# Query projection in 512 columns, and the last two groups' heads taken by token tile

## The chip, the core and the metric

The kernel runs on one core of a Trainium2 chip. The metric is the device time of one execution in microseconds. Before the change it was run three times: 1211.14, 1211.49 and 1213.31, median 1211.49. The engines are called as in the profile: PE is TensorE (matmuls; PEld its weight loads), DVE is VectorE, ACT is ScalarE, POOL is GpSimd, SP is SyncE, which issues the loads from memory.

## The reference

A two-layer decoder trunk on 512 tokens of width 1024: one mLSTM layer, then one layer of sliding-window attention with 16 query heads in 4 key-value groups, each followed by a squared-ReLU MLP and a gated embedding. The change touches the attention layer alone:

```python
def swa_sink_attention(x, pos, k_sh, v_sh, w_q, b_q, sinks, w_o, b_o):
    B, S, _ = x.shape
    nb = S // WINDOW                                    # WINDOW = 128, nb = 4
    q = partial_rope((x @ w_q + b_q).reshape(B, S, A_Q_HEADS, A_HEAD_DIM), pos)
    q = q.reshape(B, nb, WINDOW, A_KV_HEADS, A_GROUP, A_HEAD_DIM)
    kb, vb = banded(k_sh, nb), banded(v_sh, nb)
    scores = jnp.einsum('bnqkgd,bnskd->bnkgqs', q, kb).astype(jnp.float32) * (A_HEAD_DIM ** -0.5)
    ...
    m = jnp.maximum(jnp.max(scores, axis=-1), sink)
    e = jnp.exp(scores - m[..., None])
    probs = e / (jnp.sum(e, axis=-1) + jnp.exp(sink - m))[..., None]
    out = jnp.einsum('bnkgqs,bnskd->bnqkgd', probs.astype(x.dtype), vb).reshape(B, S, D_MODEL)
    return out @ w_o + b_o
```

A group has 4 query heads of 64 channels, so the queries of one group are 256 columns of x @ w_q. A token sees the 128 tokens up to itself, hence the key-value blocks of its own tile of 128 tokens and of the one before.

## The kernel before, in words

Every matrix is kept as two parts: a high part, rounded to a format that TensorE reads in one pass (`hi`), and the residue (`lo`). A product of two such matrices is three matmuls, high by high, high by low and low by high; `mm3` issues them from lines 88, 89 and 90, so that nearly all matmuls of the kernel carry those lines. A weight block of 128 x 1024 numbers (512 KB) is loaded by SyncE into one of three buffers `wraw`; ScalarE casts it to the high part (line 76) and VectorE subtracts to get the low part (line 77). Such a "split" goes into one of six buffer pairs `whi`/`wlo`.

The 512 tokens are four token tiles t = 0 to 3. The layer's input lies transposed in `XH` and `XL` (high and low), 8 blocks k of 128 channels. The attention stage runs as follows.

- Keys and values: `proj512(t, w)` takes 8 blocks x 3 matmuls of 512 columns per tile. VectorE adds the bias, rotates the keys, and four transposes through the only `tp` bank bring the keys to `KH`/`KL`.
- Queries: `q_group(gi, t, w)` does the same for one group with 256 columns. VectorE adds the bias (line 844), GpSimd rotates (lines 791 to 794), two transposes (line 848) follow, and the result goes to `QS`, which holds each head's queries as high and low part, by ScalarE copies (line 853) and VectorE subtractions (line 854).
- `attend(gi, t)`, called an attend below: 8 score matmuls into two of three `sc` banks (lines 865, 866), mask (DVE, 870), maximum (871), exponentials (ACT, 884), normalization (DVE, 888), four transposes (PE, 892), cast and residue of the probabilities `ah`, `al` (ACT 896, DVE 897), for t > 0 a triangular cut of both on GpSimd (904), then 6 (t = 0) or 12 value matmuls into a `pt` bank, and the result written over the group's queries in `QS` (ACT 915, DVE 916).
- The output projection `w_o(t, half, w)`: 24 matmuls of 512 columns per tile and half, then the residual addition (line 153) and statistics (943). The weights of the first half go into `XH` and `XL`, which can be overwritten only when the last query projection has read them; those of the second half into `whi`/`wlo`.

In the code, the four query tiles of group gi + 1 stand behind the four attends of group gi; the first half of `w_o` stands with the attends of the last group, the second half behind all attends. The emitted order is not that of the code: the framework's scheduler reorders the instructions of each engine, within what data and buffers allow, and each engine then works through its own list strictly in order. Lines 117 to 133, 141 and 145 belong to the layer norm and transposes that follow.

Of the kernel before, what the change touches and what calls it, by code (L numbers as in the profile page):

```python
# [10 lines left out]
F32 = mybir.dt.float32  # L11
# [34 lines left out]
def yoco_kernel(ctx: ExitStack, tc: tile.TileContext, A: dict, out: bass.AP):  # L46
    nc = tc.nc
    V, ACT, PE, GP = nc.vector, nc.scalar, nc.tensor, nc.gpsimd
# [30 lines left out]
    def load_w(src, n, room=None):  # L79
        raw = wpool.tile([P, 1024], F32, tag="raw", name="wraw", bufs=3)  # L80
        hi, lo = (room.tile([P, 1024], F32R, tag=f"x{x}", name=f"x{x}", bufs=4) if room else
                  wpool.tile([P, 1024], F32R, tag=f"w{x}", name=f"w{x}", bufs=6) for x in ("hi", "lo"))
        nc.sync.dma_start(raw[:, :n], src)
        split(raw[:, :n], n, hi[:, :n], lo[:, :n])
        return hi, lo

    def mm3(o, lh, ll, rh, rl, start, stop):
        PE.matmul(o, lh, rh, start=start, stop=False)  # L88
        PE.matmul(o, lh, rl, start=False, stop=False)  # L89
        PE.matmul(o, ll, rh, start=False, stop=stop)  # L90
# [18 lines left out]
    def tsl(t):  # L109
        return slice(t * P, (t + 1) * P)  # L110
# [647 lines left out]
    bq = pk.tile([P, D], F32, name="bq")  # L758
# [25 lines left out]
    pb = pool("pb", stack=bctx, side="right", reuse_waits="tile")  # L784
    def rope(x, t, nh, eng):
        tr = x[:, :, 0:ROPE].rearrange("p h (a j) -> p h a j", a=2)
        ca = cos[:, t, :].unsqueeze(1).unsqueeze(1).broadcast_to([P, nh, 2, HALF])
        sa = sin[:, t, :].unsqueeze(1).unsqueeze(1).broadcast_to([P, nh, 2, HALF])
        ta = pb.tile([P, KVH, 2, HALF], F32, tag="ta", name="ta", bufs=2)[:, :nh]
        tb = pb.tile([P, KVH, 2, HALF], F32, tag="tb", name="tb", bufs=2)[:, :nh]  # L790
        eng.tensor_mul(ta, tr, ca)
        eng.tensor_mul(tb, tr, sa)
        eng.tensor_sub(tr[:, :, 0, :], ta[:, :, 0, :], tb[:, :, 1, :])
        eng.tensor_add(tr[:, :, 1, :], ta[:, :, 1, :], tb[:, :, 0, :])
# [9 lines left out]
    w = [load_w(A["w_kv"][0, c], 1024) for c in range(4)]  # L804
# [5 lines left out]
    for t in range(NT):  # L810
        ps = proj512(t, w)
# [6 lines left out]
        pt = tp_bank()  # L818
        for h in range(KVH):
            PE.transpose(pt[:, tsl(h)], kd[:, h].rearrange("p a d -> p (a d)"), ident)  # L820
        pv = pt.rearrange("p (h s) -> p h s", s=P)
# [8 lines left out]
            put_v(vstep[t], dv)  # L830
        vlast = v

    qbank = [None]

    def q_group(gi, t, w):
        if t % 2 == 0:
            qbank[0] = mm_bank()
        ps = qbank[0][:, (t % 2) * 256:(t % 2 + 1) * 256]
        for k in range(KD):
            wh, wl = w[k // 4]  # L840
            sl = slice((k % 4) * 256, (k % 4 + 1) * 256)
            mm3(ps, XH[:, k, tsl(t)], XL[:, k, tsl(t)], wh[:, sl], wl[:, sl], k == 0, k == KD - 1)
        q = pb.tile([P, 256], F32, tag="qr", name="q", bufs=2)
        V.tensor_add(q, ps, bq[:, gi * 256:(gi + 1) * 256])  # L844
        rope(q.rearrange("p (h d) -> p h d", d=HD), t, KVH, GP)
        pt = tp_bank()
        for pr in range(2):
            PE.transpose(pt[:, tsl(pr)], q[:, tsl(pr)], ident)
        pv = pt[:, :256].rearrange("p (a s) -> p a s", a=2)
        for par in range(2):  # L850
            own, other = slice(par * HD, (par + 1) * HD), slice((1 - par) * HD, (2 - par) * HD)
            hs = slice(4 * gi + par, 4 * gi + par + 3, 2)
            ACT.copy(QS[own, hs, tsl(t)], pv[own])
            V.tensor_sub(QS[other, hs, tsl(t)], pv[own], f32(QS)[own, hs, tsl(t)])  # L854

# [60 lines left out]
        V.tensor_sub(dl, pov, f32(dh))  # L916

    def load_q(gi):
        return [load_w(A["w_q"][gi, c], 1024) for c in range(2)]

    w = load_q(0)
    for t in range(NT):
        q_group(0, t, w)
    for gi in range(KVH - 1):
        w = load_q(gi + 1)
        for t in range(NT):
            attend(gi, t)
        for t in range(NT):
            q_group(gi + 1, t, w)

    def wo_part(ps, t, w, k0, k1):
        for k in range(k0, k1):
# [16 lines left out]
        split(raw, 1024, *w[c])  # L949
    w2 = []  # L950
    for t in range(NT):
        attend(KVH - 1, t)
        w_o(t, 0, w)
        w2.append(load_w(A["w_o"][1, t], 1024))
    bctx.close()
# [24 lines left out]
def _pack(inputs):  # L980
    c = np.ascontiguousarray
    I = {k: np.asarray(v) for k, v in inputs.items()}

    def packw(W):
        return c(W.reshape(KD, P, -1, P).transpose(2, 1, 0, 3)).reshape(-1, P, KD * P)

    def packx(W, n=512):
        K, C = W.shape
        return c(W.reshape(K // 256, 2, P, C // n, n).transpose(3, 0, 2, 1, 4)).reshape(C // n, K // 256, P, 2 * n)

    def packq(W):
# [53 lines left out]
```

## Time and profile before

| | |
|---|---|
| median of three runs | 1211.49 us |
| profiled execution, its own time | 1212.01 us |
| its span, first to last instruction | 1210.3 us |
| mean granted TensorE clock | 0.994 |
| PE busy, all of the span | 1181.4 us, 98% |
| DVE busy | 878.2 us, 73% |
| ACT busy | 585.4 us, 48% |
| first query-projection matmul | 648.12 us |
| last value matmul of the last attend | 785.44 us |
| last matmul of the output projection | 808.54 us |
| first matmul of the next MLP | 811.15 us |

A timeline row reads: start, duration, engine, line, operation, output <- inputs, shape, count, and in brackets the idle time before it with what ended it. Matmuls overlap, so a matmul's price is the distance between starts, not its duration. A group row reads: line, engine, operation, names, shape, count | busy us, mean ns | idle before, releaser. The granted clock is 1.00 at full speed and 0.50 at half.

### The profile page before, as it was taken

Reading aid. Unit: us, or ns where it says so; the run is one execution under the profiler, and the core shown is the slowest. Engines: PE = TensorE matmul, PEld = TensorE weight load, DVE = VectorE, ACT = ScalarE, POOL = GpSimd, SP = SyncE. Lnnn points to the kernel's source line nnn. Section 1 sums busy time; section 2 is a strip of 40 time slices with the busy share of each in tenths; the row PEclk is TensorE's granted clock in tenths of the full one; section 3 lists DMA queues with packets and bytes.
Section 4 is the critical chain, followed back from the end, with each engine's and each line's share of the span. In section 5 each row is a group of like instructions: output and inputs, shape, how many; then the busy total and the mean of one; then the engine's idle time right before and its main releaser. Section 6 shows DMA issues by size and latency. Waiting matters only on the chain.

```text
span 1210.3 us, 15643 instructions
## 1 busy us (share of the span) xinstructions
PE 1181.4 (98%) x5918; PEld 1005.1 (83%) x5918; DVE 878.2 (73%) x1454; ACT 585.4 (48%) x1016; POOL 93.7 (8%) x190
## 2 busy tenths in 40 slices
PE   9999999999999999999999998999999999999998
PEld 8899997888888888887788897789888888888877
DVE  6556547877488499599785789676947858969974
ACT  4444544465463463564333446336646446447431
POOL 1011011100000000001201332110000000000100
PEclk9999999999999999999999999999999999999999
DMA  7322234414405316115322104151260440531411
GB/s 236 109 91 71 87 105 161 153 35 139 140 1 181 98 36 194 49 53 176 112 88 70 36 2 128 49 189 53 79 183 18 135 144 1 181 97 35 150 60 52
DMA packets 34843, 120.35 MB, mean 99 GB/s; under 512 B 3968, under 2 KB 4752, under 8 KB 34768
## 3 DMA queue, kind: packets, MB, share of 16 engines
q1 hardware_dynamic: 32688, 112.26, 29.5%
q0 software_dynamic: 2080, 7.09, 1.9%
q8 instruction: 46, 0.75, 0.3%
q14 instruction: 29, 0.24, 0.1%
HBM read 117.24 MB, written 2.10 MB: 99 GB/s over the span
## 4 chain that ended last, share of the span: by engine, by line
PE 88%; DVE 5%; issue 2%; DMA 2%; ACT 2%; POOL 0%; SPq 0%; ACTq 0%; DVEq 0%; POOLq 0%
PE mm L88 28%; PE mm L89 28%; PE mm L90 28%; PE tp L128 1%; DMA wraw<-in_w_vo_dram 1%; DVE wlo L77 1%; ACT pr L884 1%; DVE QS L854 1%; PE tp L88 0%; DVE sc L870 0%; PE tp L89 0%; PE tp L90 0%; DVE smax L871 0%; DVE al L897 0%; DVE q L844 0%
## 5 line engine op out<-in xcount | busy, mean ns | idle before, releaser
L77 DVE TENSOR_TENSOR wlo<-wraw,whi 128x1024 fp32r<-128x1024 f32 (+1 forms) x160 | 194.7, 1220 | 125.4 <-ACT whi L76 124.0
L76 ACT CAST whi<-wraw 128x1024 fp32r<-128x1024 f32 (+1 forms) x160 | 165.3, 1035 | 218.2 <-PE mm L90 98.5
L88 PE MATMUL mm<-XH,whi 128*128 128x512 f32 (+1 forms) x640 | 234.7, 369 | 2.3 <-ACT XH L132 1.7
L89 PE MATMUL mm<-XL,whi 128*128 128x512 f32 (+1 forms) x640 | 235.4, 369 | 0.0
L90 PE MATMUL mm<-XH,wlo 128*128 128x512 f32 (+1 forms) x640 | 235.1, 368 | 0.0
L88 PE MATMUL mm<-whi,XH 128*128 128x512 f32 (+2 forms) x424 | 146.9, 347 | 4.1 <-DVE q L844 2.3
L90 PE MATMUL mm<-whi,XL 128*128 128x512 f32 (+2 forms) x424 | 146.0, 345 | 0.0
L89 PE MATMUL mm<-wlo,XH 128*128 128x512 f32 (+2 forms) x424 | 145.9, 344 | 0.0
L88 PEld LDWEIGHTS mm<-XH,whi 128*128 128x128 f32 x640 | 120.1, 189 | 22.9 <-ACT XH L132 2.2
L89 PEld LDWEIGHTS mm<-XL,whi 128*128 128x128 f32 x640 | 120.6, 189 | 19.9 <-DVE XL L133 0.2
L90 PEld LDWEIGHTS mm<-XH,wlo 128*128 128x128 f32 x640 | 120.6, 189 | 19.8
L76 ACT CAST whi<-rb 128x1024 fp32r<-128x1024 f32 x80 | 84.0, 1050 | 100.4 <-PE mm L89 56.7
L77 DVE TENSOR_TENSOR wlo<-rb,whi 128x1024 fp32r<-128x1024 f32 x80 | 97.6, 1225 | 38.9 <-ACT whi L76 38.9
L88 PEld LDWEIGHTS mm<-whi,XH 128*128 128x128 f32 x424 | 80.7, 190 | 12.9 <-DVE q L844 3.7
L89 PEld LDWEIGHTS mm<-wlo,XH 128*128 128x128 f32 x424 | 80.9, 191 | 7.8 <-issue 1.5
L90 PEld LDWEIGHTS mm<-whi,XL 128*128 128x128 f32 x424 | 80.8, 191 | 6.4 <-issue 0.8
L89 PE MATMUL mm<-wlo,S23h 128*128 128x512 f32 x128 | 50.7, 396 | 0.0
L89 PE MATMUL mm<-wlo,S4Ah 128*128 128x512 f32 x128 | 50.6, 395 | 0.0
L88 PE MATMUL mm<-whi,S23h 128*128 128x512 f32 x128 | 50.6, 395 | 0.0
L88 PE MATMUL mm<-whi,S4Ah 128*128 128x512 f32 x128 | 50.6, 395 | 0.0
L90 PE MATMUL mm<-whi,S4Al 128*128 128x512 f32 x128 | 50.3, 395 | 0.0
L641 DVE TENSOR_TENSOR res<-res,mm 128x512 f32<-128x512 f32 x72 | 48.8, 685 | 1.4 <-PE mm L90 1.0
(370 smaller groups left out, 2254.6 us busy)
## 6 DMA issues: line engine op xcount, KB each, us to landing
wraw<-in_w_up_dram SPq DMA_DIRECT2D x64, 512.0 KB, 4.0
rb<-in_w_down_dram SPq DMA_DIRECT2D x48, 512.0 KB, 4.3
wraw<-in_w_down_dram SPq DMA_DIRECT2D x16, 512.0 KB, 3.7
wraw<-in_w_gate_dram SPq DMA_DIRECT2D x16, 512.0 KB, 3.7
wraw<-in_w_vo_dram SPq DMA_DIRECT2D x18, 412.0 KB, 3.5
wraw<-in_w_qk_dram SPq DMA_DIRECT2D x8, 512.0 KB, 4.4
wraw<-in_w_out_dram SPq DMA_DIRECT2D x8, 512.0 KB, 3.7
wraw<-in_w_q_dram SPq DMA_DIRECT2D x8, 512.0 KB, 3.6
```

Of the source, the lines that this page charges most:

```text
L76: ACT.copy(hi, raw)
L77: eng.tensor_sub(lo, raw, f32(hi))
L88: PE.matmul(o, lh, rh, start=start, stop=False)
L89: PE.matmul(o, lh, rl, start=False, stop=False)
L90: PE.matmul(o, ll, rh, start=False, stop=stop)
L128: PE.transpose(pt[:, tsl(j)], src[:, tsl(b + j)], ident)
L641: V.tensor_add(r[:, h], r[:, h], bank)
L854: V.tensor_sub(QS[other, hs, tsl(t)], pv[own], f32(QS)[own, hs, tsl(t)])
L884: ACT.activation(pt_[:, par, pr, :], scs[pr][:, par, :], AF.Exp, scale=ASCALE, bias=nm[:, par, pr:pr + 1], accum_out=sm[:, par, pr:pr + 1])
```

## The change

The queries of two groups are projected together: 512 columns at a time, two calls per token tile instead of four. The packed weights follow (two column halves of four blocks instead of four of two, the same bytes), the transposes come in fours, the copies into `QS` are twice as wide, and the rotary scratch `ta`/`tb` doubles. The loops change too: all weights of the second half are loaded ahead of the attends, its four tiles are written behind every second attend of groups 0 and 1, and the attends of groups 2 and 3 are written together per token tile, each pair with its `w_o(t, 0)`.

```diff
-        ta = pb.tile([P, KVH, 2, HALF], F32, tag="ta", name="ta", bufs=2)[:, :nh]
+        ta = pb.tile([P, 2 * KVH, 2, HALF], F32, tag="ta", name="ta", bufs=2)[:, :nh]
...
-    def q_group(gi, t, w):
-        if t % 2 == 0:
-            qbank[0] = mm_bank()
-        ps = qbank[0][:, (t % 2) * 256:(t % 2 + 1) * 256]
-        for k in range(KD):
-            wh, wl = w[k // 4]
-            sl = slice((k % 4) * 256, (k % 4 + 1) * 256)
-            mm3(ps, XH[:, k, tsl(t)], XL[:, k, tsl(t)], wh[:, sl], wl[:, sl], k == 0, k == KD - 1)
-        q = pb.tile([P, 256], F32, tag="qr", name="q", bufs=2)
-        V.tensor_add(q, ps, bq[:, gi * 256:(gi + 1) * 256])
-        rope(q.rearrange("p (h d) -> p h d", d=HD), t, KVH, GP)
+    def q_groups(g2, t, w):
+        ps = proj512(t, w)
+        q = pb.tile([P, 512], F32, tag="qr", name="q", bufs=2)
+        V.tensor_add(q, ps, bq[:, g2 * 512:(g2 + 1) * 512])
+        rope(q.rearrange("p (h d) -> p h d", d=HD), t, 2 * KVH, GP)
         pt = tp_bank()
-        for pr in range(2):
+        for pr in range(4):
             PE.transpose(pt[:, tsl(pr)], q[:, tsl(pr)], ident)
-        pv = pt[:, :256].rearrange("p (a s) -> p a s", a=2)
+        pv = pt.rearrange("p (a s) -> p a s", a=4)
...
-            hs = slice(4 * gi + par, 4 * gi + par + 3, 2)
+            hs = slice(8 * g2 + par, 8 * g2 + par + 7, 2)
...
-        return [load_w(A["w_q"][gi, c], 1024) for c in range(2)]
+        return [load_w(A["w_q"][gi, c], 1024) for c in range(4)]
 
     w = load_q(0)
     for t in range(NT):
-        q_group(0, t, w)
-    for gi in range(KVH - 1):
-        w = load_q(gi + 1)
+        q_groups(0, t, w)
+    w = load_q(1)
+    for gi in range(2):
         for t in range(NT):
             attend(gi, t)
-        for t in range(NT):
-            q_group(gi + 1, t, w)
+            if t % 2:
+                q_groups(1, 2 * gi + t // 2, w)
...
     for t in range(NT):
-        attend(KVH - 1, t)
+        attend(2, t)
+        attend(3, t)
         w_o(t, 0, w)
         w2.append(load_w(A["w_o"][1, t], 1024))
```

What the scheduler makes of it: the matmuls of all eight query tiles now stand ahead of the value matmuls of the third attend. Two places show the rest. In the rows a name's number tells one tile from the next.

First TensorE, at the first attend of group 1 (token tile 0). Before, its transposes (`pt_6147`) are followed by scores of a later attend (`sc_6223`, `sc_6230`), transposes of a query tile, and then the 24 matmuls of the query tile `mm_6724`, of which the last row here is the first:

```order
L892 MATMUL pt_6147<-ident_66,pr_6138 128x128 x4
L865 MATMUL sc_6223<-KH_5272,QS_5334 128x256
L866 MATMUL sc_6223<-KL_5273,QS_5334 128x256
L848 MATMUL tp_6099<-ident_66,q_6091 128x128 x2
L865 MATMUL sc_6223<-KH_5272,QS_5334 128x256
L866 MATMUL sc_6223<-KL_5273,QS_5334 128x256
L865 MATMUL sc_6230<-KH_5272,QS_5334 128x256
L866 MATMUL sc_6230<-KL_5273,QS_5334 128x256
L865 MATMUL sc_6230<-KH_5272,QS_5334 128x256
L866 MATMUL sc_6230<-KL_5273,QS_5334 128x256
L88 MATMUL mm_6724<-whi_6495,XH_64 128x256
```

Now the value matmuls of the same attend (`pt_6104`, on `ah`, `al`) stand right behind its transposes (`pt_6095`), and then two matmuls of the output projection (`mm_6482`) that read its result in `QS`:

```order
L884 MATMUL pt_6095<-ident_66,pr_6086 128x128 x4
L88 MATMUL pt_6104<-ah_6100,vo0h_5280 128x256
L89 MATMUL pt_6104<-al_6101,vo0h_5280 128x256
L90 MATMUL pt_6104<-ah_6100,vo0l_5281 128x256
L88 MATMUL pt_6104<-ah_6100,vo0h_5280 128x256
L89 MATMUL pt_6104<-al_6101,vo0h_5280 128x256
L90 MATMUL pt_6104<-ah_6100,vo0l_5281 128x256
L88 MATMUL mm_6482<-XH_64,QS_5334 128x512
L89 MATMUL mm_6482<-XL_65,QS_5334 128x512
L884 MATMUL pt_6142<-ident_66,pr_6133 128x128 x4
```

The query tile that stood between transposes and value matmuls is gone from there; it is done earlier.

Then VectorE, where the splits of the output projection's weights begin. `XL` are the residues of its first half, `wlo` those of the second. Before, the steps around them belong to attends of groups 2 and 3 (line 886 to 888 normalize), and `q_6867` is the last query tile:

```order
L77 TENSOR_TENSOR XL_65<-wraw_6886,XH_64 128x1024
L878 TENSOR_TENSOR es_6684<-sinkb_344,anm_6682 128x4
L77 TENSOR_TENSOR XL_65<-wraw_6890,XH_64 128x1024
L844 TENSOR_TENSOR q_6867<-mm_6803,bq_5276 128x256
L870 COPY_PREDICATED sc_6903<-mask_340,negc_342 128x2x128
L77 TENSOR_TENSOR XL_65<-wraw_6894,XH_64 128x1024
L871 TENSOR_REDUCE smax_6902<-sc_6903 128x2
```

Now the same splits stand among the steps of the last attend of group 0 and the first ones of group 1, with 14 of 16 attends not yet finished; `q_6351` is the last query tile:

```order
L77 TENSOR_TENSOR XL_65<-wraw_6376,XH_64 128x1024
L868 SCALAR_TENSOR_TENSOR anm_5982<-smax_5967,nsink_5278 128x4
L77 TENSOR_TENSOR XL_65<-wraw_6380,XH_64 128x1024
L77 TENSOR_TENSOR XL_65<-wraw_6384,XH_64 128x1024
L870 TENSOR_TENSOR es_5984<-sinkb_344,anm_5982 128x4
L908 TENSOR_TENSOR QS_5334<-pt_5952,QS_5334 128x2x128
L836 TENSOR_TENSOR q_6351<-mm_6326,bq_5276 128x512
L862 COPY_PREDICATED sc_6074<-mask_340,negc_342 128x2x128
```

The ten splits moved from the last third of the attends to the first. In the changed kernel the lines from 830 on are 8 lower than before: 884 is what was 892, 888 and 889 what were 896 and 897, 840 and 846 the transposes and subtractions of 848 and 854.

More of the change, by code (lines that the diff above doesn't have):

```diff
@@ L788, in rope @@
         sa = sin[:, t, :].unsqueeze(1).unsqueeze(1).broadcast_to([P, nh, 2, HALF])
-        ta = pb.tile([P, KVH, 2, HALF], F32, tag="ta", name="ta", bufs=2)[:, :nh]
-        tb = pb.tile([P, KVH, 2, HALF], F32, tag="tb", name="tb", bufs=2)[:, :nh]
+        ta = pb.tile([P, 2 * KVH, 2, HALF], F32, tag="ta", name="ta", bufs=2)[:, :nh]
+        tb = pb.tile([P, 2 * KVH, 2, HALF], F32, tag="tb", name="tb", bufs=2)[:, :nh]
         eng.tensor_mul(ta, tr, ca)
@@ L831, in yoco_kernel @@
         vlast = v
-    qbank = [None]
-    def q_group(gi, t, w):
-        if t % 2 == 0:
-            qbank[0] = mm_bank()
-        ps = qbank[0][:, (t % 2) * 256:(t % 2 + 1) * 256]
-        for k in range(KD):
-            wh, wl = w[k // 4]
-            sl = slice((k % 4) * 256, (k % 4 + 1) * 256)
-            mm3(ps, XH[:, k, tsl(t)], XL[:, k, tsl(t)], wh[:, sl], wl[:, sl], k == 0, k == KD - 1)
-        q = pb.tile([P, 256], F32, tag="qr", name="q", bufs=2)
-        V.tensor_add(q, ps, bq[:, gi * 256:(gi + 1) * 256])
-        rope(q.rearrange("p (h d) -> p h d", d=HD), t, KVH, GP)
+    def q_groups(g2, t, w):
[3 more added lines that the diff above has]
+        rope(q.rearrange("p (h d) -> p h d", d=HD), t, 2 * KVH, GP)
         pt = tp_bank()
-        for pr in range(2):
+        for pr in range(4):
             PE.transpose(pt[:, tsl(pr)], q[:, tsl(pr)], ident)
-        pv = pt[:, :256].rearrange("p (a s) -> p a s", a=2)
+        pv = pt.rearrange("p (a s) -> p a s", a=4)
         for par in range(2):
             own, other = slice(par * HD, (par + 1) * HD), slice((1 - par) * HD, (2 - par) * HD)
-            hs = slice(4 * gi + par, 4 * gi + par + 3, 2)
+            hs = slice(8 * g2 + par, 8 * g2 + par + 7, 2)
             ACT.copy(QS[own, hs, tsl(t)], pv[own])
@@ L989, in packx @@
         return c(W.reshape(K // 256, 2, P, C // n, n).transpose(3, 0, 2, 1, 4)).reshape(C // n, K // 256, P, 2 * n)
-    def packq(W):
-        return c(W.reshape(2, 4, P, KVH, 256).transpose(3, 0, 2, 1, 4)).reshape(KVH, 2, P, 1024)
     x = I["x"][0]
@@ L1012, in _pack @@
         "kv_b": I["kv_b"],
-        "w_q": packq(I["b_w_q"][0]),
+        "w_q": packx(I["b_w_q"][0]),
         "b_b_q": c(I["b_b_q"][0]),
```

## The prediction

> **What bounds the kernel now.** I read the page first, then the stage of the change in windows of 10 us, then single rows of the TensorE timeline.
>
> ```profile
> span 1210.3 us, 15643 instructions
> PE 1181.4 (98%) x5918; PEld 1005.1 (83%) x5918; DVE 878.2 (73%) x1454; ACT 585.4 (48%) x1016; POOL 93.7 (8%) x190
> ...
> PE 88%; DVE 5%; issue 2%; DMA 2%; ACT 2%; POOL 0%; SPq 0%; ACTq 0%; DVEq 0%; POOLq 0%
> ```
>
> TensorE carries 88% of the chain that ended last, so whatever shortens or fills its queue counts. The windows (columns: stretch, length, then busy time and instruction count of PE, PEld, DVE, ACT, POOL, then granted clock, DMA share, GB/s) show where the attention stage leaves it idle:
>
> ```profile
> 650.00:730.00 80.00, 74.33 (x591) 71.85 (x590) 56.50 (x157) 36.53 (x138) 24.66 (x68) 0.98 0.11 33
> 670.00:680.00 10.00, 8.04 (x54) 7.83 (x54) 6.08 (x21) 6.05 (x23) 2.12 (x8) 0.83 0.13 49
> 730.00:740.00 10.00, 8.93 (x69) 8.32 (x68) 9.64 (x26) 8.15 (x27) 2.42 (x7) 1.00 0.06 11
> 750.00:760.00 10.00, 6.29 (x35) 5.43 (x32) 9.80 (x19) 7.15 (x20) 1.27 (x2) 0.83 0.71 212
> 760.00:770.00 10.00, 8.54 (x44) 7.12 (x45) 8.66 (x25) 4.32 (x20) 1.27 (x2) 0.83 0.17 58
> 780.00:790.00 10.00, 10.00 (x51) 8.34 (x50) 2.32 (x4) 0.37 (x1) 1.57 (x3) 1.00 0.40 141
> ```
>
> From 650 to 730 TensorE has projections to put between the steps of an attend and is 93% busy, VectorE 71% (56.5 of 80). From 730 to 760 VectorE is at 96 to 98%, and TensorE starves; at 780 the reverse holds. So the stage, from the first projection matmul at 648.1 to the first MLP matmul at 811.15, is limited by two engines in turn, and the change alters when.
>
> **The prices.** Pitches are start to start, since durations overlap.
>
> ```profile
> 638.11 0.39 PE L88 MATMUL mm<-whi,XH 128*128 128x512 f32 x1
> 643.34 0.39 PE L90 MATMUL mm<-whi,XL 128*128 128x512 f32 x1
> ...
> 648.12 0.28 PE L88 MATMUL mm<-whi,XH 128*128 128x256 f32 x1
> ...
> 666.89 0.28 PE L89 MATMUL mm<-wlo,XH 128*128 128x256 f32 x1
> 669.51 0.28 PE L90 MATMUL mm<-whi,XL 128*128 128x256 f32 x1
> ...
> 678.76 0.60 PE L892 MATMUL pt<-ident,pr 128*128 128x128 f32 x4
> 679.12 0.36 PE L88 MATMUL mm<-whi,XH 128*128 128x256 f32 x1
> ...
> 770.19 0.40 PE L89 MATMUL mm<-XL,QS 128*128 128x512 f32 x1
> 774.63 0.39 PE L90 MATMUL mm<-XH,QS 128*128 128x512 f32 x1
> ```
>
> 638.11 to 643.34 are the 24 matmuls of one tile: 5.23 over 23 steps, 0.2274 each at 512 columns. 666.89 to 669.51 are 23 matmuls: 2.62 over 22, 0.119 at 256. 770.19 to 774.63 are 20 of the output projection: 4.44 over 19, 0.233. Four transposes take 0.36 and slow the next matmul by about 0.09: 0.45.
>
> *Width.* 384 projection matmuls of 256 columns become 192 of 512: 384 x 0.119 = 45.7 against 192 x 0.2274 = 43.7, so 2.0 off TensorE. The Trainium skill ("TensorE: Matmul & The Clock Gate", Back-to-back issue gap) gives a warm gap of N/2.4 + 2.5 ns, 109 and 216 ns, by which I estimate a saving of only 0.5 us, and 1209.7 for the whole. The trace does not agree: 256 columns take 0.119.
>
> *VectorE, ScalarE, GpSimd, DMA.*
>
> ```profile
> L77 DVE TENSOR_TENSOR wlo<-wraw,whi 128x1024 fp32r<-128x1024 f32 x11 | 13.9, 1272 | 2.4 <-ACT whi L76 2.2
> L854 DVE TENSOR_TENSOR QS<-tp,QS 64x256 fp32r<-64x256 f32 x32 | 13.5, 422 | 1.5 <-ACT QS L853 0.4
> ...
> L844 DVE TENSOR_TENSOR q<-mm,bq 128x256 f32<-128x256 f32 x16 | 6.7, 421 | 10.0 <-PE mm L90 3.8 <-PE tp L848 3.4 <-issue 2.8
> L813 DVE TENSOR_TENSOR kv<-mm,kvb 128x512 f32<-128x512 f32 x1 | 0.7, 684 | 0.0
> ...
> L897 DVE TENSOR_TENSOR al<-pt,ah 128x512 fp32r<-128x512 f32 x15 | 10.2, 677 | 1.1 <-ACT ah L896 1.1
> ...
> L76 ACT CAST whi<-wraw 128x1024 fp32r<-128x1024 f32 x10 | 10.5, 1051 | 6.8 <-DMA wraw<-in_w_up_dram 2.0 <-DMA wraw<-in_w_o_dram 1.7 <-DMA wraw<-in_w_q_dram 1.6
> ...
> L896 ACT CAST ah<-pt 128x512 fp32r<-128x512 f32 x15 | 8.9, 596 | 1.6 <-PE pt L892 1.4
> ...
> L792 POOL TENSOR_TENSOR tb<-q,sin 128x64 f32<-128x64 f32 x16 | 6.2, 385 | 0.0
> ...
> wraw<-in_w_o_dram SPq DMA_DIRECT2D x8, 512.0 KB, 3.8
> ```
>
> 16 bias additions and 32 residue subtractions (20.2) become 8 and 16 of twice the width, priced at the 512-column kv addition (0.684): 24 x 0.684 = 16.4, 3.8 less. ScalarE's copies shrink likewise beside free time. The rotary work halves in instructions; a tile's transposes stand at least 19 matmuls (4.3) after its bias addition, which covers about 2 us of GpSimd. The eight 512 KB loads of w_q stay, issued earlier on SyncE; two more splits must be ready inside the first q tile (for its matmuls 13 and 19), and the slots they reuse come free inside the key-value tile before it, a tile's length (5.4) or more earlier, enough for a cast (1.05) and a split (1.27). I cost these at zero; without the cover a tile waits 1 to 2 us once.
>
> *Order, stage A.* The built order puts all eight q tiles before most attends: 8 x 24 x 0.2274 = 43.7, with ten blocks of transposes (4.5), 36 score matmuls and 18 value matmuls (54 x 0.119 = 6.4), together 54.6 from 648.1, plus 1.0 for two waits I found following the order: 703.7. Before, this much TensorE work loses time (670 to 680: 2.0 idle and a clock of 0.83).
>
> *Stage B1.* At 703.7 only two attends of sixteen are complete, and the projections that used to fill in are used up. What comes next is VectorE's.
>
> ```profile
> 737.20 1.22 DVE L77 TENSOR_TENSOR XL<-wraw,XH 128x1024 fp32r<-128x1024 f32 x1
> 738.34 0.16 DVE L878 TENSOR_TENSOR es<-sinkb,anm 128x4 f32<-128x4 f32 x1
> ...
> 763.73 0.42 DVE L870 COPY_PREDICATED sc<-mask,sc 128x256 f32<-128x256 uint8 x1
> 764.06 0.42 DVE L916 TENSOR_TENSOR QS<-pt,QS 128x256 fp32r<-128x256 f32 x1
> ```
>
> A split holds VectorE 1.14 (737.20 to 738.34), a 256-column step about 0.35 (763.73 to 764.06). The order puts ten splits (11.4) among the next 49 VectorE instructions, up to the first probabilities of group 1; the other 39 sum to 14.7 at such pitches. The first split waits for the last q tile's sixth matmul and a cast, about 697.1; 697.1 + 26.1 = 723.2, which I take as 723.4. TensorE has 10.4 of work there between 703.7 and 723.4 and idles 9.3. Before, the same ten splits ran from 737.2 to about 759 with more filler.
>
> *Stage B2*, up to the last attend's value matmuls: 118 output-projection matmuls (27.5), 126 value and 68 score matmuls (23.1), 12 blocks of transposes (5.4): 56.0. Waits come on top, because an attend's transposes are now followed at once by its value matmuls, which need a cast and a subtraction first, as these rows show:
>
> ```profile
> 752.57 0.38 PE L88 MATMUL pt<-ah,vo2h 128*128 128x256 f32 x1 [1.64 <-ACT ah L896]
> 755.01 0.44 PE L89 MATMUL pt<-al,vo2h 128*128 128x256 f32 x1 [1.82 <-DVE al L897]
> 755.24 0.42 PE L90 MATMUL pt<-ah,vo2l 128*128 128x256 f32 x1
> 757.17 0.41 PE L90 MATMUL pt<-bh,vs3l 128*128 128x256 f32 x1
> ...
> 750.00:764.00 14.00, 8.97 (x46) 7.63 (x44) 13.65 (x31) 8.69 (x26) 1.27 (x2) 0.81 0.63 192
> 756.00:758.00 2.00, 2.00 (x11) 1.98 (x11) 1.94 (x5) 1.35 (x2) 0.00 (x0) 0.50 0.69 234
> ```
>
> Lower bound 0. Upper bound 11: the share of idle time of 750 to 764 (5.0 of 14, 36%) on the six attends in which little output projection stands between, with 19.6 of TensorE work: 19.6 / 0.64 - 19.6. Following the order attend by attend with a cast (0.60), a subtraction (0.68) and what stands between, I get 2.2 at the first (nothing between), 0.9 until its result is back in QS for the next output matmuls, 1.0 over the next two, 0.4 at the fourth, 1.7 and 0.8 at the two of tile 0: 7.0, nearer the upper end. Then the clock: after gaps of 1.64 and 1.82 the pitch nearly doubles (755.24 to 757.17, ten rows, 1.93 over 9 steps: 0.214; granted clock 0.50). A mean of 0.83 over ten microseconds is 3.4 at half clock, which loses about 1.6. I take two such stretches (3.2), as 750 to 770 had, bounds 0 and four (6.4). Last value matmul: 723.4 + 56.0 + 7.0 + 3.2 = 789.6.
>
> *Stage C.*
>
> ```profile
> 785.56 0.40 PE L90 MATMUL mm<-whi,QS 128*128 128x512 f32 x1
> ...
> 808.77 1.03 PE L128 MATMUL tp<-ident,res 128*128 128x128 f32 x8
> ...
> 811.15 0.36 PE L88 MATMUL mm<-XH,whi 128*128 128x256 f32 x1
> ```
>
> Before, 94 output-projection matmuls stand behind the last value matmul (785.56), and the MLP starts at 811.15. Afterwards 62 are left: 32 x 0.233 = 7.5 less; transposes and their waits I count as equal. So 811.15 becomes 811.15 + (789.6 - 785.6) - 7.5 = 807.7, 3.4 less; what follows is the same work. The profiled execution took 1212.0 (span 1210.3), 0.5 above the median of 1211.5: I forecast 1208.2 against that median.
>
> **The rivals.**
>
> 1. *TensorE stays fed* (0.15). With VectorE's 3.8 us less and all q ready, waits in B2 shrink to 1 and one cold stretch remains: 6.0 + 1.6 = 7.6 less, 1200.6; with neither waits nor a lower clock 10.2 less, 1198. For it: VectorE ran at 96 to 98% without gaps. Against: the rows at 752 and 755.
> 2. *The clock stays full* (0.10), waits as forecast: 3.2 less, 1205.0. Against it stands the row of 756 to 758. The Trainium skill ("TensorE: Matmul & The Clock Gate", HAM oscillation) asks for no idle gap above about 3.4 us, and none here is so long; the trace does not agree, its clock fell after two gaps below 2 us.
> 3. *Starvation wins: slower* (0.23). Place: the first six attends of B2. If they idle 36% (4.0 more than I took) and two more cold stretches follow (3.2), it ends 7.2 later: 1215.4. It decides from waits plus cold of 13.6 (I have 10.2): above this the kernel is slower.
> 4. *Only a reshuffle* (0.07): the idle of 670 to 760 reappears in B1 whole, and the 2.0 of width is lost in the new wait: 1211.5. The code's interleaving "one q tile per two attends" does not survive the scheduling, which speaks for it.
>
> **How the numbers follow.** The forecast's case has 0.45. About 0.2% (2.4 us) is what a measurement can tell from no change. Its own range is 1205 to 1212: 0.25 of it faster, 0.20 within 2.4. Faster: 0.25 + 0.15 + 0.10 = 0.50; same: 0.20 + 0.07 = 0.27; slower 0.23. For 8 in 10 the range runs from 1199, inside rival 1, to 1216, just past rival 3's time.
>
> **What would show it.** Right: no projection matmul of 256 columns at L88 to L90 from 648; last q tile near 704; window 705 to 722 with TensorE near half busy, VectorE above 90%; last value matmul near 790; MLP start near 808. Wrong: waits in stage A above 3 (splits of q weights late), B1 ending after 727, or a granted clock below 0.8 through 720 to 750.

## The result and the profile after

The changed kernel takes 1218.37 us (median of 4 runs, 1216.80 to 1219.22) beside 1211.32 us for the kernel before on the same chip: ratio 1.0057, 95% interval 1.0037 to 1.0078. It is 7 us slower, where 3.3 us faster was forecast, and lies above the forecast's range. The profiled execution took 1217.92, a span of 1216.0.

The page of the changed kernel, the same lines as of before:

```profile
span 1216.0 us, 15173 instructions
...
PE 1183.0 (97%) x5726; PEld 998.6 (82%) x5726; DVE 874.6 (72%) x1430; ACT 586.3 (48%) x1000; POOL 86.7 (7%) x158
...
PE 86%; DVE 6%; DMA 3%; issue 2%; ACT 2%; POOL 0%; SPq 0%; DVEq 0%; ACTq 0%; POOLq 0%
```

VectorE's busy time fell by 3.6 (878.2 to 874.6; 3.8 was forecast), 192 matmuls fewer are there, and still TensorE's share of the chain fell by two points, one of which went to DMA. The windows of the changed kernel, columns as before:

```profile
700.00:710.00 10.00, 9.30 (x51) 7.58 (x50) 9.84 (x21) 7.38 (x17) 2.88 (x7) 1.00 0.48 175
710.00:720.00 10.00, 3.83 (x18) 3.40 (x18) 9.06 (x16) 7.75 (x17) 0.69 (x2) 0.83 0.66 192
720.00:730.00 10.00, 7.14 (x34) 6.08 (x35) 9.68 (x23) 5.74 (x21) 0.59 (x1) 0.70 0.43 142
730.00:740.00 10.00, 10.00 (x60) 9.12 (x59) 6.90 (x21) 5.07 (x26) 2.95 (x4) 0.79 0.00 1
...
800.00:810.00 10.00, 8.44 (x43) 6.54 (x41) 10.00 (x13) 5.66 (x7) 0.34 (x1) 1.00 0.39 140
810.00:820.00 10.00, 7.21 (x33) 6.62 (x34) 9.52 (x14) 2.60 (x3) 3.70 (x2) 0.66 0.64 200
```

Two places lose time. At 710 to 730 TensorE starves beside a nearly full VectorE, as forecast. At 800 to 820 it starves again, and that was not forecast. Before, the same stretch has TensorE nearly full, with the full clock:

```profile
800.00:810.00 10.00, 9.81 (x53) 7.99 (x51) 9.31 (x12) 5.93 (x9) 2.47 (x2) 1.00 0.02 3
810.00:820.00 10.00, 9.26 (x78) 9.26 (x79) 9.93 (x16) 6.32 (x11) 1.46 (x1) 1.00 0.65 209
```

The rows of TensorE that mark the way (changed kernel, timeline):

```profile
703.04 0.40 PE L90 MATMUL mm<-whi,XL 128*128 128x512 f32 x1
...
714.37 0.58 PE L857 MATMUL sc<-KH,QS 128*128 128x256 f32 x1 [4.86 <-ACT pr L876]
...
724.74 0.60 PE L884 MATMUL pt<-ident,pr 128*128 128x128 f32 x4
...
791.61 0.28 PE L90 MATMUL pt<-bh,vs3l 128*128 128x256 f32 x1
...
805.92 0.39 PE L90 MATMUL mm<-whi,QS 128*128 128x512 f32 x1
806.15 1.73 PE L128 MATMUL tp<-ident,res 128*128 128x128 f32 x12
...
809.35 0.63 PE L88 MATMUL mm<-XH,whi 128*128 128x256 f32 x3 [1.47 <-ACT XH L132]
812.49 0.39 PE L88 MATMUL mm<-XH,whi 128*128 128x256 f32 x1 [2.52 <-DVE res L153]
...
820.28 0.36 PE L88 MATMUL mm<-XH,whi 128*128 128x256 f32 x1
```

The last query tile ends at 703.3, the last value matmul is at 791.6 (before 785.4), and the last output-projection matmul starts at 805.9, which is 2.6 *earlier* than before (808.54). Up to here the change is ahead. Then the MLP, which before flowed from 811.15 on, makes three matmuls, waits, runs at half clock (0.21 from row to row) and flows only from 820.28. The wait of 2.52 is for the residual addition (L153), which stands in VectorE's queue behind this (changed kernel: GpSimd's and VectorE's rows, then two steps of the chain that ended last):

```profile
792.07 0.63 POOL L120 DMA_DIRECT2D bc<-in_mix_ln_g_dram  x1 [3.53 <-PE pt L90]
...
799.85 2.48 DVE L144 SCALAR_TENSOR_TENSOR res<-res,mv,bc 128x1024 f32<-128x1024 f32 x2 [4.20 <-DMA bc<-in_mix_ln_g_dram]
```

```profile
792.07 7.75 DMA bc<-in_mix_ln_g_dram
799.85 2.48 DVE res L144 x2
```

The load of the layer norm's gain goes to memory that the attends hold, so it is issued when the last value matmul is done, takes 7.75 us, and holds VectorE's queue for 4.2 us; after that VectorE is busy almost without a gap (10.00 and 9.52). Three splits of MLP weights (807.14 to 811.75, 3.4 us together) also stand in its queue ahead of that residual addition; no run moved them. Before, the same load stands at these places:

```profile
785.90 0.60 POOL L120 DMA_DIRECT2D bc<-in_mix_ln_g_dram  x1 [5.47 <-PE pt L90]
...
793.54 1.28 DVE L144 SCALAR_TENSOR_TENSOR res<-res,mv,bc 128x1024 f32<-128x1024 f32 x1 [2.20 <-DMA bc<-in_mix_ln_g_dram]
```

The wait was there before, 2.20 us long, but 94 output-projection matmuls (22 us) stood behind the last value matmul and ran beside it. The changed kernel has 62 (14.4 us) behind a value matmul that comes 6.2 later.

### The profile page after: what moved, and what is told of

It is laid out like the page before. It is cut to its first block, busy times and chain, and to the rows that moved or that the text cites. A ratio compares the mean times of both kernels' runs of the same rounds, so it can differ in the third digit from the quotient of the medians.

```text
span 1216.0 us, 15173 instructions
## 1 busy us (share of the span) xinstructions
PE 1183.0 (97%) x5726; PEld 998.6 (82%) x5726; DVE 874.6 (72%) x1430; ACT 586.3 (48%) x1000; POOL 86.7 (7%) x158
## 4 chain that ended last, share of the span: by engine, by line
PE 86%; DVE 6%; DMA 3%; issue 2%; ACT 2%; POOL 0%; SPq 0%; DVEq 0%; ACTq 0%; POOLq 0%
PE mm L89 27%; PE mm L90 27%; PE mm L88 27%; PE tp L128 1%; DVE wlo L77 1%; DMA wraw<-in_w_vo_dram 1%; DMA bc<-in_mix_ln_g_dram 1%; DVE res L144 1%; ACT whi L76 1%; PE sc L857 1%; PE tp L88 0%; PE sc L858 0%; PE pt L89 0%; PE tp L90 0%; PE tp L89 0%
## 5 line engine op out<-in xcount | busy, mean ns | idle before, releaser
L88 PE MATMUL mm<-whi,XH 128*128 128x512 f32 (+2 forms) x360 | 134.1, 373 | 1.6 <-ACT XH L132 1.1
L89 PE MATMUL mm<-wlo,XH 128*128 128x512 f32 (+2 forms) x360 | 134.0, 373 | 0.0
L90 PE MATMUL mm<-whi,XL 128*128 128x512 f32 (+2 forms) x360 | 134.0, 374 | 0.0
L88 PEld LDWEIGHTS mm<-whi,XH 128*128 128x128 f32 x360 | 67.6, 188 | 11.3 <-ACT XH L132 2.5
L89 PEld LDWEIGHTS mm<-wlo,XH 128*128 128x128 f32 x360 | 67.7, 188 | 10.1 <-issue 1.5
L90 PEld LDWEIGHTS mm<-whi,XL 128*128 128x128 f32 x360 | 67.7, 188 | 8.8 <-issue 0.8
L90 PE MATMUL mm<-whi,S23l 128*128 128x512 f32 x128 | 49.6, 395 | 0.0
```

## The experiments

Theory 1: the arrival of gain and bias holds stage C. Theory 2: the starved attends, which put the last value matmul later, carry the loss. Each run was timed in turn with the kernel before on its own chip (1211.3 to 1212.1 us there), so differences in us between runs are differences of these ratios times 1211.5. The positions are those of each run's one profile.

| run | median us | ratio to before (95%) | last value matmul | gain issued | first gain step | first MLP ReLU |
|---|---|---|---|---|---|---|
| before | 1211.3 | 1 | 785.44 | 785.90 | 793.54 | 816.77 |
| after | 1218.4 | 1.0057 (1.0037–1.0078) | 791.61 | 792.07 | 799.85 | 822.36 |
| 1 after, early load | 1209.4 | 0.9982 (0.9974–0.9991) | 792.06 | 774.19 | 788.27 | 812.31 |
| 2 before, early load | 1210.9 | 0.9994 (0.9984–1.0003) | 783.22 | 765.72 | 789.02 | 811.40 |
| 3 width alone | 1217.8 | 1.0054 (1.0041–1.0066) | 788.98 | 789.44 | 796.96 | 821.76 |
| 4 order alone | 1221.5 | 1.0087 (1.0073–1.0101) | 795.63 | 796.10 | 803.97 | 825.70 |
| 5 load at 788 | 1210.2 | 0.9986 (0.9977–0.9994) | 792.62 | 787.80 | 791.81 | 812.89 |
| 6 width, early load | 1212.5 | 1.0006 (0.9994–1.0017) | 790.99 | 778.32 | 793.51 | 815.69 |
| 7 order, early load | 1214.9 | 1.0021 (1.0009–1.0033) | 796.30 | 776.66 | 792.55 | 816.53 |
| 8 run 1, splits spread | 1207.7 | 0.9963 (0.9949–0.9977) | 790.85 | 771.13 | 787.06 | 811.09 |
| 9 own tiles, load late | 1215.8 | 1.0031 (1.0018–1.0043) | 789.69 | 794.31 | 798.48 | 820.25 |
| 10 run 1, transposes last | 1211.8 | 1.0000 (0.9990–1.0010) | 791.37 | 773.48 | 787.58 | 816.83 |
| 11 run 1, queries as filler | 1219.8 | 1.0062 (1.0050–1.0075) | 802.94 | 783.64 | 798.37 | 822.46 |
| 12 before, load late | 1212.3 | 1.0006 (0.9996–1.0016) | 784.48 | 790.97 | 794.93 | 818.27 |
| 13 after, down loads held | 1212.2 | 1.0000 (0.9991–1.0009) | 789.06 | 789.52 | 793.27 | 816.71 |
| 14 run 1, splits later still | 1206.8 | 0.9955 (0.9943–0.9968) | 789.01 | 766.83 | 788.88 | 810.37 |

From the first ReLU to the end of the span it is 391 to 396 us, so some of what is won at the ReLU is given back in the MLP's first tiles, and the medians decide.

**1 and 2: the load, early.** The edit, the same in both kernels but for the select that it names and the line with "bufs", which only the changed kernel needs for room:

```diff
-    kvb = pk.tile([P, 512], F32, name="kvb")
+    kvb = pk.tile([P, D], F32, name="kvb")          # used as [:, :512] until here
...
-            dv = pb.tile(..., bufs=2)                # and ta
+            dv = pb.tile(..., bufs=1)
...
+    g, b = bq, kvb
+    with tc.issue_after(sel[3, 2].ins):              # GpSimd's select of attend(3, 2); before: (3, 1)
+        nc.gpsimd.dma_start(g, A["mix_ln_g"][1].partition_broadcast(P))
+        nc.gpsimd.dma_start(b, A["mix_ln_b"][1].partition_broadcast(P))
     bctx.close()
-    kctx.close()
...
-    open_mid("right")
-    g, b = bcast(A["mix_ln_g"][1]), bcast(A["mix_ln_b"][1])
     for t in range(NT):
         w_o(t, 1, w2)
         ln_finish(t, sts[t], g, b)
+    kctx.close()
+    open_mid("right")
```

> The changed kernel, except that the layer norm's gain and bias go into two tiles that exist already (the query bias and the key-value bias, whose last readers are long done) and are loaded from the last attends but one on, instead of into memory that the last attend's value matmuls release. The order of all engines up to the last attend stays as it is; only stage C is re-sorted. Theory 1 (the load's place): VectorE's wait of 4.2 us at L144 and what precedes it go, the layer norms start 4 to 6 us earlier, and so does the MLP's full flow (820.3): 1212.5 to 1214.5 us; if nothing else holds stage C, the MLP starts 2.6 us after the last output-projection matmul (805.9) and the time is 1210. Theory 2 (starved attends): the last value matmul, which is 6.2 us later than before, carries the loss, and VectorE's list of stage C is full whenever the load comes: at most 1 us less, 1217.4 to 1218.4.

> The kernel before with the same early load of the layer norm's gain and bias. Theory 1: 94 output-projection matmuls (22 us) behind the last value matmul cover the load there, TensorE idles only 0.93 us ahead of the MLP: 0 to 1.5 us less, 1209.8 to 1211.3. Theory 2: no change, 1211.3.

The first run's stage C, that is from the last value matmul to the MLP (VectorE's row of the first gain step, then TensorE's rows):

```profile
788.27 1.27 DVE L144 SCALAR_TENSOR_TENSOR res<-res,mv,bq 128x1024 f32<-128x1024 f32 x1
...
808.12 0.40 PE L90 MATMUL mm<-whi,QS 128*128 128x512 f32 x1
808.36 1.03 PE L128 MATMUL tp<-ident,res 128*128 128x128 f32 x8
809.15 0.36 PE L88 MATMUL mm<-XH,whi 128*128 128x256 f32 x1
```

No wait at L144, and the MLP flows 1.0 after the last output-projection matmul. The last value matmul is where the changed kernel has it (792.06, 791.61), and yet 9.1 us are gone (1.0057 to 0.9982). Theory 2 falls: at the same starvation the kernel is faster than before. In the kernel before the same edit is worth 0.7 us, which its interval does not tell from nothing. Against that kernel with its early load (run 2, timed on the same chip) the change gains 1.5 us (1209.4 against 1210.9); the two intervals overlap a little.

The edit moves something else too. The attends' memory is now given back only behind the layer norms, and with it six loads of down-projection weights go later. In the changed kernel SyncE starts them beside the gain's load:

```profile
791.14 2.84 SPq L486 DMA_DIRECT2D rb<-in_w_down_dram  x6
```

In run 1 they start at 815.50, and in every run with the gain in a tile of its own (all but 3, 4 and 13) at 808 or later. Run 1 thus changes when the gain's load starts and what moves beside it; run 13 changes only the second.

**3 and 4: width alone, order alone.** Run 3 is the changed kernel with

```diff
     for t in range(NT):
         attend(2, t)
+    for t in range(NT):
         attend(3, t)
         w_o(t, 0, w)
```

Run 4 is the kernel before, with `attend(gi, t)` for groups 0 and 1 only in the old loop, and

```diff
-        attend(KVH - 1, t)
+        attend(2, t)
+        attend(3, t)
         w_o(t, 0, w)
```

> The projection of the change (512 columns, two groups together) with the loops of the kernel before behind it: all attends of group 2 first, then by token tile the attend of group 3 and the output projection's first half. 113 output-projection matmuls stand ahead of the last value matmul and 79 behind it (changed kernel 130 and 62, kernel before 98 and 94). Theory 1: the last value matmul comes 17 x 0.233 = 4.0 us earlier than in the changed kernel, near 787.7, and the MLP follows it at the same distance: about 1214.4. Theory 2: the starved place between 710 and 730 is shared with the changed kernel, and the same total of TensorE work follows: 1217 to 1219.

> The kernel before (queries of one group in 256 columns, the old loops over groups 0 and 1) with the changed loop over token tiles: attends of groups 2 and 3, then the output projection's first half. 62 output-projection matmuls are left behind the last value matmul. Theory 1: the last value matmul comes between 789 and 793 (7.5 us of output projection ahead of it, less up to 4 of waits that it fills), and the MLP follows it as before: 1215 to 1219. Theory 2: the query tiles of 256 columns are still there as filler among the attends, so nothing starves more than before: 1208 to 1212.

Either half of the change alone is as slow as the whole, or slower. Run 4 lies 2.5 beyond theory 1's range and far outside theory 2's. Run 3 lies 3.4 above theory 1's number and inside theory 2's range: I had let the MLP follow the last value matmul at a fixed distance, and it followed later. Run 3's profile (GpSimd, VectorE) shows the load's wait again, longer than in the changed kernel:

```profile
789.44 0.60 POOL L120 DMA_DIRECT2D bc<-in_mix_ln_g_dram  x1 [5.42 <-PE pt L90]
...
796.96 1.29 DVE L144 SCALAR_TENSOR_TENSOR res<-res,mv,bc 128x1024 f32<-128x1024 f32 x1 [5.38 <-DMA bc<-in_mix_ln_g_dram]
```

**6 and 7: the same two with the early load** (the edit of run 1 on the kernels of runs 3 and 4).

> Width alone (512-column query projection, old loops behind it) together with the early load of gain and bias. If the loss of the width alone (1217.8) is the load again (its wait at L144 was 5.38 us): 1209 to 1211. If it is the starved place between 710 and 730: 1215 to 1217.

> Order alone (256-column query tiles, attends of groups 2 and 3 by token tile) together with the early load. Order alone took 1221.5, with the last value matmul at 795.6, 3.6 us after that of the changed kernel. With the load out of the way that distance should be what is left against the first experiment (1209.4): about 1213. If stage C is held by something else: 1217 or more.

Both lose most of their excess: width 5.8 us (1.0054 to 1.0006), order 8.0 (1.0087 to 1.0021). Each missed its number by 1.5 to 2 us on the slow side. With the load out of the way the four kernels stand at 0.9994 (neither), 1.0006 (width), 1.0021 (order) and 0.9982 (both): only the two together are clear of the kernel before. Why each alone is a little worse was not followed further.

**5, 9 and 10: arrival, release or sorting?** Run 5 is run 1 with the load behind GpSimd's last select, run 9 with the load behind the statistics of the second token tile (in tiles that need no release), run 10 with the early load, but all transposes of the layer norms behind the last output-projection matmul, as the changed kernel orders them:

```diff
-    with tc.issue_after(sel[3, 2].ins):     # run 5
+    with tc.issue_after(sel[3, 3].ins):
...
-    with tc.issue_after(sel[3, 2].ins):     # run 9, after the statistics of tiles 0 and 1
+    with tc.issue_after(last_rs[0].ins):
...
-        ln_finish(t, sts[t], g, b)          # run 10
+    for t in range(NT):
+        with tc.issue_after(lastpe[0].ins): ln_finish(t, sts[t], g, b)
```

(`last_rs[0]` is GpSimd's last step of the latest statistics, `lastpe[0]` the last output-projection matmul.)

> As the first experiment (changed kernel, gain and bias into the old bias tiles), but the two loads are queued on GpSimd behind the selects of the very last attend (near 787) instead of those of two attends earlier (774). Theory 1 (the load's arrival holds stage C): it lands near 794.5, between the first experiment's (by 782) and the changed kernel's (799.85), so VectorE's first gain step moves from 788.3 to about 794.5 and the time lies between the two: 1211 to 1215 us, or as little as 1210 if stage C has slack of that size. Rival (the way stage C is sorted made the gain, not the load): 1209.4, as in the first experiment, with the wait at L144 as long as it likes.

> As the first experiment (gain and bias in tiles of their own, so that no memory has to be released for them), but the two loads are queued on GpSimd behind the layer norm statistics of the second token tile, near 796, so that they land between 800 and 804, as late as in the changed kernel or later. Theory 1 (the load's arrival is what stage C waits for): as slow as the changed kernel or slower, 1218 to 1222. Rival (something else in the release of the attends' memory, not the arrival of gain and bias): fast as the first experiment, 1209 to 1211.

> As the first experiment, with the early load, but TensorE's order in stage C is that of the changed kernel again: all transposes of the layer norms' results behind the last output-projection matmul. Theory 1 (arrival): the results are ready early, so after the last matmul near 805.9 stand only the transposes of the first two tiles (2 us) with their copies and subtractions: MLP in flow near 810 to 812, 1210 to 1213. Rival (the better sorting made the gain of 9 us): 1216 or more.

Runs 5 and 9, issue and first gain step in each:

```profile
787.80 0.60 POOL L950 DMA_DIRECT2D bq<-in_mix_ln_g_dram  x1
...
791.81 1.28 DVE L144 SCALAR_TENSOR_TENSOR res<-res,mv,bq 128x1024 f32<-128x1024 f32 x1 [2.90 <-DMA bq<-in_mix_ln_g_dram]
```

```profile
794.31 0.63 POOL L964 DMA_DIRECT2D bq<-in_mix_ln_g_dram  x1
...
798.48 2.48 DVE L147 SCALAR_TENSOR_TENSOR res<-res,mv,bq 128x1024 f32<-128x1024 f32 x2 [0.53 <-DMA bq<-in_mix_ln_g_dram]
```

Run 5 was meant to land near 794.5; it landed at 791.8, because the load, without the six beside it, takes 4.0 us here and not 7.75, so it tells less of a late load than planned: 0.5 us slower than run 1 with 3.5 us more lateness. Run 9, without any release to wait for, is 5.9 us slower than run 1, so a late arrival costs time without the release. Not all of the 5.9 is the arrival: twelve transposes stand behind the last output-projection matmul in run 9 too, as in run 10. Against run 10 it is 3.8 us slower. It misses the 1218 that I expected by 2 us, with a first gain step 1.4 ahead of the changed kernel's. (Its runs spread from 1212.6 to 1218.2, and the profiled one took 1213.4.) Run 10 shows that sorting has a part: 2.2 us for the transposes' place, with the load early (first gain step 787.58). Five kernels have the same program up to stage C; by lateness they stand in this order:

| first gain step | 788.3 (run 1) | 791.8 (run 5) | 793.3 (run 13) | 798.5 (run 9) | 799.9 (after) |
|---|---|---|---|---|---|
| ratio to before | 0.9982 | 0.9986 | 1.0000 | 1.0031 | 1.0057 |

Up to about 792 the intervals show no cost of lateness, and from there to 799.9 the time grows by 8.6 us in 8.0. That is not the arrival alone: in run 9 and the changed kernel all transposes stand behind the last output-projection matmul, in the other three some stand ahead of it.

**12: the kernel before with a late load**: run 2 with the load behind `last_rs[0]` of the first token tile's statistics.

> The kernel before with gain and bias in tiles of their own, and their loads queued on GpSimd behind the layer norm statistics of the first token tile, near 789 to 791, some 4 to 6 us after where the kernel before issues them (785.9). Theory 1: its 22 us of output projection behind the last value matmul cover the load as it is with little to spare (TensorE waits 0.93 us), so 2 to 5 us slower: 1213 to 1216. Rival: 1210.5 to 1212, no change, since stage C has slack.

The rival held but for 0.3: no change against before, 1.5 us more than run 2. The load was issued 5.1 later but took 4.0 instead of 7.6, so it arrived only 1.4 later. The cover of 94 matmuls was not tested as hard as meant.

**13: why the load takes 7.75 us.** When the attends' memory comes free, SyncE starts six loads of down-projection weights into it, whose first use is a cast at 838. One edit to the changed kernel:

```diff
-            nc.sync.dma_start(r, src[0][src[1] + c])
+            with (tc.issue_after(n_up[0].ins) if held[0] else ExitStack()): nc.sync.dma_start(r, src[0][src[1] + c])
```

(`n_up[0]` is the seventh load of up-projection weights; `held[0]` is true in the second MLP's first quarter only.)

> The changed kernel with one edit: the six loads of down-projection weights that start when the attends' memory is released (791, 3 MB, not needed before the MLP's second product) are queued on SyncE behind the seventh up-projection load. Gain and bias keep their place and still wait for the release. If sharing the DMA engines is what makes the load take 7.8 us: it takes 4 to 4.5, the first gain step starts near 796 instead of 799.85, and the time falls by 2 to 4 us, to 1214 to 1216.5. If the load's own length or the release is all of it: 1218, no change.

The DMA issues of 780 to 812 (count, size, median us from issue to landing), the changed kernel and run 13:

```profile
rb<-in_w_down_dram SPq DMA_DIRECT2D x6, 512.0 KB, 7.4
...
bc<-in_mix_ln_g_dram POOLq DMA_DIRECT2D x1, 512.0 KB, 7.8
```

```profile
bc<-in_mix_ln_g_dram POOLq DMA_DIRECT2D x1, 512.0 KB, 3.7
```

The gain lands in 3.7 us, and the kernel takes 1212.2: 6.9 us back, more than the 2 to 4 expected, since the first gain step came 6.6 earlier (4.0 of it by the shorter load, 2.5 by an earlier last value matmul in this profile, 789.06, which the edit does not explain) and the transposes were sorted forward with it: twelve stand ahead of the last output-projection matmul. How much of the 6.9 is the shorter load and how much that order was not separated. The Trainium skill ("DMA: Bandwidth & Descriptors", Issuing engines are not separate DMA queues) says that transfers from the sync and GpSimd queues run on the same 16 engines and interleave; the trace agrees, 7.8 us beside the six and 3.7 without them.

**8, 14 and 11: the starved stretch.** Run 8 is run 1 with

```diff
-        w2.append(load_w(A["w_o"][1, t], 1024))
+        with tc.issue_after(vend[1, t].ins): w2.append(load_w(A["w_o"][1, t], 1024))
```

(`vend[g, t]` is VectorE's last instruction of that attend); run 14 has `vend[2, t]`. Run 11 is run 1 with

```diff
-                q_groups(1, 2 * gi + t // 2, w)
+                with tc.issue_after(pend[gi, t].ins): q_groups(1, 2 * gi + t // 2, w)
```

(`pend[g, t]` is the last transpose of that attend's probabilities).

> The first experiment's kernel, and in it the residue subtractions of the output projection's second-half weights are queued on VectorE one by one behind the attends of group 1, so that six splits (6 x 1.14 = 6.8 us) leave the stretch between 710 and 730, where VectorE is 95% busy and TensorE half idle. If starvation there has a price: the stretch shortens by 4 to 6 us, part of it comes back where the splits now stand (VectorE 75 to 80% busy there), the last value matmul comes 2 to 5 us before 792.1, and the time is 1205 to 1207.5. If VectorE's total binds up to the last attends: 1209.4, unchanged.

> As the eighth run, but the residue subtractions of the second-half weights are queued behind the attends of group 2, one per token tile, rather than group 1: still later, with 48 output-projection matmuls instead of 62 behind the last value matmul. If the starved stretch is all that counts: another 1 to 2 us, 1205.5 to 1207. If the subtractions now collide with the layer norms at the end (three stand behind the last token tile's attends): 1209 or more.

> As the first experiment, and each query tile of the second pair is queued on TensorE behind the transposes of an attend of groups 0 and 1 (one tile per two attends, as the code is written), instead of being sorted ahead of them. If TensorE starves in 710 to 730 because its query work is spent: the waits there (6.1 for free score banks, 5.3 for the parts of the probabilities) shrink by half, and the last value matmul comes 4 to 6 us earlier, 786 to 788: 1203 to 1206. Against it: the output projection's splits start later, since the query tiles read the same memory until then; if VectorE's total is what counts: 1208 to 1210.

The stretch in runs 1 and 14 (columns as above):

```profile
710.00:720.00 10.00, 4.51 (x20) 3.45 (x18) 9.31 (x17) 6.84 (x16) 0.79 (x3) 0.83 0.67 225
720.00:730.00 10.00, 5.36 (x34) 4.18 (x34) 9.75 (x24) 6.56 (x19) 1.27 (x2) 0.99 0.54 161
```

```profile
710.00:720.00 10.00, 7.38 (x37) 6.88 (x37) 5.50 (x14) 7.31 (x25) 1.27 (x2) 0.66 0.00 1
720.00:730.00 10.00, 7.55 (x51) 6.21 (x50) 9.64 (x28) 5.70 (x23) 1.27 (x2) 1.00 0.00 0
```

With the splits away TensorE is busy for 14.9 us there instead of 9.9, part of it at a lower clock. Less of it arrives at the end: run 8 gains 2.3 us and misses its range by 0.2 (its last value matmul came 1.2 earlier, where 2 to 5 were expected). Run 14 gains 3.3, as expected, and is the fastest of all, 0.45% below before (0.9955, 0.9943 to 0.9968). Run 11 is a plain miss: 9.7 us slower than run 1. Two rows of its TensorE and one of its windows:

```profile
676.09 0.38 PE L857 MATMUL sc<-KH,QS 128*128 128x256 f32 x1 [1.74 <-DVE QS L846]
...
704.79 1.09 PE L884 MATMUL pt<-ident,pr 128*128 128x128 f32 x4 [3.38 <-DVE es L870]
```

```profile
750.00:760.00 10.00, 5.40 (x27) 4.22 (x26) 9.44 (x18) 6.64 (x12) 0.00 (x0) 0.78 0.74 242
```

Holding the query tiles back made TensorE wait at 676 and 704, where the changed kernel has no gap, and at 750, where the splits now pile up (those of the first half write into `XH` and `XL`, which the query tiles read until then). That TensorE starves because its query work is spent is not borne out, though this run moved the splits as well; that VectorE's splits stand there in one block has a price, by runs 8 and 14.

## Why the prediction was wrong, and where it was right

- *Width, VectorE, stage A* held. Stage A was to end at 703.7 and ended at 703.3; VectorE's busy time fell by 3.6 against 3.8; the split weights caused no wait there.
- *Stage B1* held nearly. The first probabilities of group 1 were expected at 723.4, and their transposes stand at 724.74; TensorE's waits between 704 and 724 are 7.4 (9.3 of idle was forecast), mainly the 4.86 at 714.37.
- *Stage B2* was 2 us short in the profiled run: 791.6 against 789.6, of which 1.3 came from B1. Six profiles with this program put the last value matmul between 789.06 and 792.62, mean 791.1. The waits I followed (7.0) are of the right size: from 724 to 792 TensorE waits 5.3 us in the changed kernel, 3.9 of it for the two parts of the probabilities, and 7.2 in run 1.
- *The clock's term (3.2) was wrong in kind.* The windows 0.83, 0.70 and 0.79 fall short of the full clock by 6.8 us, as much as four stretches of 3.4 at half clock where I took two, and no cost of it shows. Runs 1 and 5 have the same program there; the clock was 0.99 at 720 to 730 in the one and 0.59 in the other (below), and their last value matmuls lie 0.56 apart. Over 710 to 740 the six profiles fall short by 3.4 (run 1) to 8.5 (runs 5 and 9), and run 9 ends earlier (789.69) than run 1. TensorE's speed did not set the stage's end there: at a lower clock it was busy longer (7.39 against 5.36) and idle less. By these profiles rival 2 had little to win.

```profile
720.00:730.00 10.00, 7.39 (x33) 6.13 (x33) 9.57 (x22) 5.68 (x17) 0.65 (x2) 0.59 0.46 150
```

- *Stage C is the step that failed*: "transposes and their waits I count as equal", and so 32 matmuls fewer behind the last value matmul were 7.5 us less. The 7.5 held: the last output-projection matmul starts 14.3 after the last value matmul, before 23.1 (8.8 less, since twelve transposes that stood between now stand behind). The waits were not equal: from that matmul to the MLP's flow 14.4 us pass (805.92 to 820.28), before 2.6. I took TensorE's queue for the path because it was full before. It was full because 22 us of matmuls covered a second path that starts at the same instant: release, load, layer norms, MLP. With 14.4 us of cover the second path ends last. TensorE's rows said nothing of it; VectorE's row at 793.54, with its wait of 2.20 for the load, did, and the prediction follows TensorE alone in stage C. With the load early the changed kernel takes 1209.4 (1208.2 was forecast), but that is 1.5 less than the kernel before with the same early load, where TensorE's terms gave 3.3.
- *A reading of the profile before* was too broad: "from 730 to 760 VectorE is at 96 to 98%, and TensorE starves" passes over 740 to 750, where VectorE is at 92% and TensorE is full. No term of the sum hangs on it.
- *Rival 3* named the sign and a time (1215.4) for another reason. Its place, the first attends of B2, is not where the loss lies: run 1 waits there at least as long as the changed kernel (7.2 against 5.3 us) and is faster than before. That the sign came out as in rival 3 is luck.

What is known of the 9.1 us between the changed kernel and run 1: 6.9 go when the load's neighbours are held back (run 13), and 2.2 depend on where TensorE's transposes stand (run 10). These are not two shares of the 9.1, for in run 13 the transposes were sorted forward too. The release itself was never taken away alone, with the six loads left at 791.

## What to carry to other kernels

When a change shortens the work behind an event, list everything else that starts at that event and follow each to the point where they meet: the next longest may become the path, and a wait that an engine off the path shows before the change tells where to look (2.20 us here; it does not tell the size of the loss). Here a tile whose memory came from a pool that was just closing could not be loaded ahead; a load that the next stage needs at once deserves memory of its own, and prefetches that start at the same release are better queued behind it. A low clock on TensorE showed no cost here while another engine set the end of the stage.

## What the runs showed of the hardware

- A 512 KB load, one row broadcast to all partitions, took 3.7 to 4.3 us from issue to landing without the six other 512 KB loads beside it (runs 1, 2 and 5 to 14) and 7.5 to 7.9 when they started within three microseconds of it (before 7.6, after 7.8, run 3 7.5, run 4 7.9).
- The granted clock of the same program in the same ten microseconds was 0.99 in one profile and 0.59 in another (runs 1 and 5). The Trainium skill ("TensorE: Matmul & The Clock Gate", HAM oscillation) asks for no idle gap above some 3.4 us; the trace agrees in part: the one wait above that in the changed kernel from 700 to 830 is the 4.86 at 714, the low clock goes on to 740 behind waits of 0.5 to 1.1 only, and at 814 the pitch is that of half clock (0.21) behind waits of 1.47 and 2.52.
